# Four shared buffers, decays from ScalarE's queue, a tap on ScalarE and two moved matmul jobs in a hybrid encoder

## The chip, the cores and the metric

The kernel runs on one core of a Trainium2 chip. The metric is the device time of one execution in microseconds (us). The kernel before takes 1397.3 us, the median of three runs (1395.79 to 1398.4).

## What is computed

Two layers work on 256 tokens of width 1024 in float32. In each, one projection of the normalized input feeds three branches: a gated width-3 convolution A, a dilated attention B with 16 heads, and a bidirectional state-space branch C with 32 heads of width 64 (SSD). Their outputs go through W_a, W_b and W_c, are gated and summed ("mix"), go through W_o, and a squared-ReLU MLP follows. The parts that the change touches are these:

```
xbc = silu(depthwise_conv_centred(xbc, conv_w) + conv_b)       # 5 taps, 24 blocks of 128 channels
cum = cumsum(la, axis=2)                                       # per chunk of 128 tokens, per head
seg = cum[:, :, :, None] - cum[:, :, None, :]
decay = exp(where(tri, seg, -inf))
y_diag = einsum("bclsgr,bcsgrp->bclgrp", cb[..., None] * decay, xd)
x = x + (g_a * y_a + g_b * y_b + g_c * y_c) @ w_o
```

The kernel writes a head's SSD, both directions and both chunks, as one 256x256 matrix of decays times C·B, which multiplies x.

## The kernel before, in words

Each weight block (128x1024, 512 KB) is loaded by a request on SP's queue (`load`, L158), and is split into a rounded part wh on ScalarE and a remainder wl on VectorE (`split_to`, L173 and L174). Four raw and three split blocks are held. Three matmuls for each piece (L181, L183, L184 with 256 columns; L218 to L220 in `wide` with 512) give the product.

TensorE's order is written out by hand. `product` and `wide` call `tick()` every 12 or 6 matmuls, and small jobs (generators in `Slots`) wake at their tick: the SSD (`ssd_job`, `ssd_pair`), the attention (`attention`), and the turning of the mix (`turn_job`). A number that a job yields, or with which it is launched, is a count of ticks. The other engines' order is made by a scheduler, which puts instructions into each in-order queue by its own estimate of when they are ready.

Per layer the stages are: values; the projections with the convolutions (`conv5`); the first gate and W_a, beside which nine of the 16 pairs of SSD heads run; queries and keys with the attention; the second gate and W_b with the other seven pairs; z, the third gate and W_c; W_o; the MLP.

`conv5` (L466) sums five taps on VectorE, the centre one first (L470), into a tile cacc, of which there are two; ScalarE's Silu (L475) follows. `decays` (L477) asks for a head's summed decays in four 256 KB tiles cr through SP's queue, where weight blocks also wait. `ssd_pair` (L484) takes two heads: GpSimd adds the mask into a tile lg, of which there are two (L495); VectorE adds it to the rest of cr (L496); ScalarE takes exponentials of lg (L498) and of cr (L502, into ar); VectorE adds and multiplies them (L506, L507). Six ticks later TensorE multiplies (L512) into the one bank oy, and VectorE empties it (L516). The attention's output matmul (L642) uses the same bank, and ScalarE and VectorE empty it (L645, L646). Each group of four pairs first turns its x with two fills of the one bank pt (L534, emptied by L537), and the turning of the attention's scores uses that bank too (L631, emptied into prt by L636). `turn_job(0)` turns the first half of the mix (L717) two ticks after the first half of W_c is through, while VectorE still adds that half to the mix (L667, L668).

Of the kernel before, what the change touches and what calls it, by code (L numbers as in the profile page):

```python
# [18 lines left out]
P = 128  # L19
# [69 lines left out]
def trunk_kernel(ctx: ExitStack, tc: tile.TileContext, xT, pos, wst, wdt, small, fin, consts, out):  # L89
# [268 lines left out]
    def layer(l, xw, squares):  # L358
        prm = sm[l]

        def col(c):
            return prm[:, c : c + 1]

        st = Stream(l)
        done = set()


        uh, ul = u = big("uh"), big("ul")
# [2 lines left out]
        def norm_job():  # L371
            norm["rs"] = rs = squares.mean(D, True)
            yield 3
            pn = bcast_tokens(rs)
            for kt in range(KT):
                uf = tmp.tile([P, S], F32, name="uf", tag="cacc", bufs=2)
                DVE.scalar_tensor_tensor(uf, x[:, kt, :], col(C_MIXW + kt), pn, ALU.mult, ALU.mult)
                split_to(uh[:, kt, :], ul[:, kt, :], uf)
            if l == 0:
                rotary_tables()  # L380
            done.add("u")
# [81 lines left out]
        def xsr(ct):  # L463
            return xs[ct // 8][:, ct % 8, :]

        def conv5(raw, wct):  # L466

            acc = tmp.tile([P, S], F32, name="cacc", bufs=2)
            wc = C_SCW + 5 * wct
            DVE.tensor_scalar(acc, raw, col(wc + 2), col(C_SCB + wct), ALU.mult, ALU.add)  # L470
            for j in (0, 1, 3, 4):
                lo, hi = max(0, 2 - j), min(S, S + 2 - j)
                DVE.scalar_tensor_tensor(acc[:, lo:hi], raw[:, lo + j - 2 : hi + j - 2], col(wc + j),  # L473
                                         acc[:, lo:hi], ALU.mult, ALU.add)
            ACT.activation(raw, acc, AF.Silu)  # L475

        def decays(h):  # L477

            cr = tmp.tile([P, 4, P], F32, name="cr", bufs=CUM_BUFS)
            nc.sync.dma_start(cr.rearrange("p (d t) l -> p d (t l)", d=2),  # L480
                              ssd["cum"][h : h + 1].to_broadcast([P, 2, S]))
            return cr

        def ssd_pair(g, hp, xt, cb, ar, crs):  # L484
            bs = ssd["bs"]
            ct = 4 * g + hp
            av = []
            for j in range(2):
                h = 2 * ct + j
                cr = crs[j]  # L490
                a = ar[(2 * ct + j) % len(ar)]
                av.append(a)
                lg = tmp.tile([P, 2, P], F32, name="lg", bufs=2)

                POOL.tensor_tensor(lg, cr[:, 0::3, :], msk, ALU.add)  # L495
                DVE.tensor_tensor(cr[:, 1:3, :], cr[:, 1:3, :], msk, ALU.add)  # L496
                for t in range(2):
                    ACT.activation(lg[:, t, :], lg[:, t, :], AF.Exp,  # L498
                                   bias=bs[:, t, 32 * (1 - t) + h : 32 * (1 - t) + h + 1])

                for t in range(2):
                    ACT.activation(a[:, t * 256 : t * 256 + 256],  # L502
                                   cr[:, 2 - 2 * t : 4 - 2 * t, :].rearrange("p t l -> p (t l)"), AF.Exp,
                                   bias=bs[:, t, 32 * t + h : 32 * t + h + 1])
                ad = a.rearrange("p (q l) -> p q l", q=4)[:, 0::3, :]
                DVE.tensor_tensor(ad, ad, lg, ALU.add)  # L506
                DVE.tensor_tensor(a, a, cb, ALU.mult)  # L507
            yield Y_DELAY
            py = bank("oy", 1)
            for t in range(2):  # L510
                for j in range(2):
                    PE.matmul(py[j * 64 : j * 64 + 64, 0:256],  # L512
                              xt[:, t, hp * 128 + j * 64 : hp * 128 + j * 64 + 64],
                              av[j][:, t * 256 : t * 256 + 256], start=t == 0, stop=t == 1)
            xv = xsr(ct)
            DVE.scalar_tensor_tensor(xv, xv, col(C_SD + ct), py[:, 0:256], ALU.mult, ALU.add)  # L516
            done.add(("y", ct))

        def ssd_job():
            ar4 = big("ar", F32).rearrange("p (b c) s -> p b (c s)", b=4)  # L520
            ar2 = tmp.tile([P, 2, 512], F32, name="ar2")
            ar = [ar4[:, i, :] for i in range(4)] + [ar2[:, i, :] for i in range(2)]
            def heads(ct):
                return [decays(2 * ct + j) for j in range(2)] if ct < 16 else None

            nxt = [heads(0)]
            for g in range(4):
                bc = bcs[g]
                xt = tmp.tile([P, 2, 512], F32, name="xt", bufs=2)
                cb = tmp.tile([P, 512], F32, name="cb", bufs=2)  # L530
                for t in range(2):
                    tx = bank("pt", 1)
                    for j in range(4):
                        PE.transpose(tx[:, j * 128 : j * 128 + 128],  # L534
                                     xsr(4 * g + j)[:, t * 128 : 128 + t * 128], ident)
                    with tc.high_priority(offset=PRIO_W):
                        ACT.copy(xt[:, t, :], tx)  # L537
                    if t == 0:
                        pb = bank("s", 2)
                        for i in range(2):  # L540
                            PE.matmul(pb[:, i * 256 : i * 256 + 256], bc[:, 0, i * 128 : i * 128 + 128],
                                      bc[:, 1, :], start=True, stop=True)
                        with tc.high_priority(offset=PRIO_W):
                            ACT.copy(cb, pb)
                        yield 1
                for hp in range(4):
                    while "qk" in done and ("att", SSD_RESUME) not in done:
                        yield 1
                    crs = nxt[0]
                    nxt[0] = heads(4 * g + hp + 1)  # L550
                    slots.launch(ssd_pair(g, hp, xt, cb, ar, crs), 1)
                    yield SSD_EVERY


# [2 lines left out]
        for g in range(4):  # L557
            bc = tmp.tile([P, 2, 256], F32, name="bc", bufs=4)
            bcs.append(bc)
            ACT.copy(bc, chunks(st, 2, u))  # L560
            conv5(bc[:, 0, :], 16 + g)
            conv5(bc[:, 1, :], 20 + g)
            av = []
            for q in range(2):
                t_ = t2k("ca")
                ACT.copy(t_, chunks(st, 2, u))
                av.append(t_)
                c0 = 4 * g + 2 * q
                ACT.copy(xs[c0 // 8][:, c0 % 8 : c0 % 8 + 2, :], chunks(st, 2, u))
                for h in range(2):  # L570
                    conv5(xsr(c0 + h), c0 + h)
            bgt, ca = av
            cx = t2k("cx")
            DVE.tensor_tensor(cx, chunks(st, 2, u), ca, ALU.mult)
            for h in range(2):
                wc = C_CONVA + 3 * (2 * g + h)
                DVE.tensor_scalar(ca[:, h, :], cx[:, h, :], col(wc + 1), None, ALU.mult)
                DVE.scalar_tensor_tensor(ca[:, h, 1:S], cx[:, h, 0 : S - 1], col(wc), ca[:, h, 1:S],
                                         ALU.mult, ALU.add)
                DVE.scalar_tensor_tensor(ca[:, h, 0 : S - 1], cx[:, h, 1:S], col(wc + 2), ca[:, h, 0 : S - 1],  # L580
                                         ALU.mult, ALU.add)
            DVE.tensor_tensor(ca, ca, bgt, ALU.mult)
            split_to(ah[:, 2 * g : 2 * g + 2, :], al[:, 2 * g : 2 * g + 2, :], ca)
# [17 lines left out]
        def attention(c, qk):  # L601
# [25 lines left out]
            for j in range(2):  # L627
                tp = bank("pt", 1)
                for kb in range(2):
                    for t in range(2):  # L630
                        PE.transpose(tp[:, kb * 256 + t * 128 : kb * 256 + t * 128 + 128],  # L631
                                     scs[j][:, t, kb * 128 : kb * 128 + 128], ident)
                prt = tmp.tile([P, 512], F32, name="prt", bufs=2)
                prts.append(prt)
                with tc.high_priority(offset=PRIO_W):
                    ACT.copy(prt, tp)  # L636
                yield 2 + j
            po = bank("oy", 1)
            for kb in range(2):
                for j in range(2):  # L640
# [92 lines left out]
        def c_sink(t, c, ps):  # L733
            with tc.high_priority(offset=2 * PRIO_W if c else 0):
                add_c(t, c, ps)
            if t == 1 and c == 0:
                slots.launch(turn_job(0), 2)

        wide(st, [(ch[0], cl[0]), (ch[1], cl[1])], c_sink, 1)

# [206 lines left out]
```

## Time and profile before

| | |
|---|---|
| median of three runs | 1397.3 us |
| the profiled execution | 1397.34 us |
| its span, first to last instruction | 1395.6 us |
| mean granted TensorE clock | 0.996 |
| TensorE busy | 1362.4 us |
| VectorE busy | 1022.7 us |
| ScalarE busy | 874.4 us |

TensorE is busy in nearly all slices, so what counts is where it stands still. The two layers lie about 690 us apart: what the text says of a place at 234 us in the first layer has its counterpart near 924 us in the second.

### The profile page before, as it was taken

The numbers are of one execution on the slowest core, as the hardware profiler recorded it, in microseconds if no ns is written. First come the engines' busy times: TensorE is split into PE (matmuls) and PEld (weight loads), VectorE is DVE, ScalarE is ACT, GpSimd is POOL, SyncE is SP. The second block draws the span as 40 slices with busy tenths as digits, with TensorE's granted clock in tenths as the row PEclk, the third lists the DMA queues.
The fourth block names the chain that finished last, engine by engine and source line by source line (L and its number), as shares of the span: only waits on it lengthen the run. The fifth ranks groups of instructions, "written<-read, shape, count | busy, mean of one in ns | idle before, by whom it ended". The sixth has DMA issues, their size and how long they took to land.

```text
span 1395.6 us, 24040 instructions
## 1 busy us (share of the span) xinstructions
PE 1362.4 (98%) x9396; PEld 1229.6 (88%) x9396; DVE 1022.7 (73%) x1662; ACT 874.4 (63%) x1387; POOL 76.1 (5%) x73
## 2 busy tenths in 40 slices
PE   7999999999999999999999999999999999999997
PEld 6999986887898799999989999778878987999886
DVE  7989989975776476655579898889767765766454
ACT  6667877777576355554456687767775763555443
POOL 0000113100100000000000001220010000000000
PEclk9999999999999999999999999999999999999999
DMA  7555666534555555555555665664344555555553
GB/s 257 183 198 198 199 201 208 168 116 137 165 179 168 166 183 180 182 183 185 183 186 177 202 212 196 200 197 152 122 151 159 174 174 179 191 182 183 174 192 115
DMA packets 73698, 249.71 MB, mean 179 GB/s; under 512 B 8240, under 2 KB 8496, under 8 KB 73584
## 3 DMA queue, kind: packets, MB, share of 16 engines
q1 hardware_dynamic: 72912, 246.78, 53.9%
q8 instruction: 73, 1.20, 0.3%
q0 software_dynamic: 240, 0.77, 0.2%
q10 hardware_dynamic: 432, 0.64, 0.1%
q14 instruction: 41, 0.34, 0.1%
HBM read 246.97 MB, written 1.18 MB: 178 GB/s over the span
## 4 chain that ended last, share of the span: by engine, by line
PE 82%; DVE 9%; ACT 3%; DMA 3%; issue 2%; POOL 0%; SPq 0%; ACTq 0%; DVEq 0%; POOLq 0%
PE mm L181 16%; PE mm L184 16%; PE mm L183 16%; PE mm L218 9%; PE mm L219 9%; PE mm L220 9%; DVE wl L174 4%; DMA cr<-cumd 2%; ACT wh L173 2%; PE oy L512 2%; DVE cacc L473 1%; PE oy L642 1%; PE pt L631 1%; PE s L607 1%; DVE cr L496 0%
## 5 line engine op out<-in xcount | busy, mean ns | idle before, releaser
L174 DVE TENSOR_TENSOR wl<-raw,wh 128x1024 fp32r<-128x1024 f32 (+1 forms) x436 | 532.8, 1223 | 285.7 <-ACT wh L173 282.9
L173 ACT CAST wh<-raw 128x1024 fp32r<-128x1024 f32 (+1 forms) x436 | 454.3, 1043 | 390.5 <-PE mm L183 179.8
L181 PE MATMUL mm<-uh,wh 128*128 128x256 f32 x1296 | 371.9, 287 | 0.0
L184 PE MATMUL mm<-uh,wl 128*128 128x256 f32 x1296 | 366.9, 283 | 3.0 <-DVE wl L174 3.0
L183 PE MATMUL mm<-ul,wh 128*128 128x256 f32 x1296 | 366.6, 283 | 0.0
L181 PEld LDWEIGHTS mm<-uh,wh 128*128 128x128 f32 x1296 | 248.3, 192 | 9.6 <-issue 9.4
L184 PEld LDWEIGHTS mm<-uh,wl 128*128 128x128 f32 x1296 | 248.4, 192 | 3.8 <-DVE wl L174 3.8
L183 PEld LDWEIGHTS mm<-ul,wh 128*128 128x128 f32 x1296 | 248.5, 192 | 0.2
L183 PE MATMUL mm<-xl,wh 128*128 128x256 f32 x512 | 145.1, 283 | 0.2
L181 PE MATMUL mm<-xh,wh 128*128 128x256 f32 x512 | 145.1, 283 | 0.0
L184 PE MATMUL mm<-xh,wl 128*128 128x256 f32 x512 | 144.9, 283 | 0.0
L495 POOL TENSOR_TENSOR lg<-cr,cst 128x256 f32<-128x256 f32 x64 | 74.0, 1169 | 969.8 <-DVE cacc L473 430.9
L183 PEld LDWEIGHTS mm<-xl,wh 128*128 128x128 f32 x512 | 98.3, 192 | 0.6 <-DVE xl L281 0.6
L181 PEld LDWEIGHTS mm<-xh,wh 128*128 128x128 f32 x512 | 98.3, 192 | 0.0
L184 PEld LDWEIGHTS mm<-xh,wl 128*128 128x128 f32 x512 | 98.3, 192 | 0.0
L218 PE MATMUL mm<-wh,uh 128*128 128x512 f32 x192 | 79.5, 414 | 0.0
L219 PE MATMUL mm<-wl,uh 128*128 128x512 f32 x192 | 75.2, 392 | 0.0
L220 PE MATMUL mm<-wh,ul 128*128 128x512 f32 x192 | 75.1, 391 | 0.0
L181 PE MATMUL mm<-sh,wh 128*128 128x256 f32 x256 | 72.4, 283 | 0.0
L183 PE MATMUL mm<-sl,wh 128*128 128x256 f32 x256 | 72.4, 283 | 0.0
L184 PE MATMUL mm<-sh,wl 128*128 128x256 f32 x256 | 72.4, 283 | 0.0
L498 ACT ACTIVATE lg<-lg,bs 128x128 f32<-128x128 f32 x128 | 45.6, 396 | 39.4 <-POOL lg L495 39.0
(217 smaller groups left out, 2443.0 us busy)
## 6 DMA issues: line engine op xcount, KB each, us to landing
raw<-in_wst_dram SPq DMA_DIRECT2D x432, 512.0 KB, 3.8
cr<-cumd SPq DMA_DIRECT2D x64, 256.0 KB, 4.4
x<-in_xT_dram SPq DMA_DIRECT2D x4, 256.0 KB, 6.6
raw<-in_wdt_dram SPq DMA_DIRECT2D x2, 512.0 KB, 4.1
cst<-in_consts_dram SPq DMA_DIRECT2D x1, 706.0 KB, 8.3
finw<-in_fin_dram POOLq DMA_DIRECT2D x1, 512.0 KB, 5.3
out_dram<-xtok ACTq DMA_DIRECT2D x2, 256.0 KB, 2.6
out_dram<-xtok SPq DMA_DIRECT2D x2, 256.0 KB, 2.6
```

The costliest lines, as they stand in the source:

```text
L173: ACT.copy(dst_h, src)
L174: DVE.tensor_tensor(dst_l, src, dst_h.bitcast(F32), ALU.subtract)
L181: PE.matmul(ps, wh[:, kt, :], rh[:, kt, :], start=first and kt == kts[0], stop=False, skip_group_check=True)
L183: PE.matmul(ps, wh[:, kt, :], rl[:, kt, :], start=False, stop=False, skip_group_check=True)
L184: PE.matmul(ps, wl[:, kt, :], rh[:, kt, :], start=False, stop=last and kt == kts[-1], skip_group_check=True)
L218: PE.matmul(ps[t], rh, wh[:, k, :], start=kt == 0, stop=False)
L219: PE.matmul(ps[t], rh, wl[:, k, :], start=False, stop=False)
L220: PE.matmul(ps[t], rl, wh[:, k, :], start=False, stop=kt == rows - 1)
L473: DVE.scalar_tensor_tensor(acc[:, lo:hi], raw[:, lo + j - 2 : hi + j - 2], col(wc + j), acc[:, lo:hi], ALU.mult, ALU.add)
L495: POOL.tensor_tensor(lg, cr[:, 0::3, :], msk, ALU.add)
L498: ACT.activation(lg[:, t, :], lg[:, t, :], AF.Exp, bias=bs[:, t, 32 * (1 - t) + h : 32 * (1 - t) + h + 1])
L512: PE.matmul(py[j * 64 : j * 64 + 64, 0:256], xt[:, t, hp * 128 + j * 64 : hp * 128 + j * 64 + 64], av[j][:, t * 256 : t * 256 + 256], star ...
```

## The change

- The tile cacc, the normalization's uf and the SSD's lg now share one set of four buffers (before: two for cacc and uf together, two for lg).
- A head's decays are requested on ScalarE's queue. Two pairs are asked for when the SSD begins, and each pair asks for the second one after it, at its own end.
- The SSD's and the attention's output matmuls wait until two ticks after the last taker of bank oy.
- The mix is first turned six ticks, not two, after the first half of W_c.
- The centre tap with its bias is one ScalarE activation that reads the projection's bank, instead of a VectorE operation that reads the copy.

```
-                uf = tmp.tile([P, S], F32, name="uf", tag="cacc", bufs=2)
+                uf = tmp.tile([P, S], F32, name="uf", tag="cacc", bufs=4)
...
-            acc = tmp.tile([P, S], F32, name="cacc", bufs=2)
+            acc = tmp.tile([P, S], F32, name="cacc", bufs=4)
             wc = C_SCW + 5 * wct
-            DVE.tensor_scalar(acc, raw, col(wc + 2), col(C_SCB + wct), ALU.mult, ALU.add)
+            ACT.activation(acc, ps, AF.Identity, bias=col(C_SCB + wct), scale=col(wc + 2))
...
-            nc.sync.dma_start(cr.rearrange("p (d t) l -> p d (t l)", d=2),
+            nc.scalar.dma_start(cr.rearrange("p (d t) l -> p d (t l)", d=2),
                               ssd["cum"][h : h + 1].to_broadcast([P, 2, S]))
...
-                lg = tmp.tile([P, 2, P], F32, name="lg", bufs=2)
+                lg = tmp.tile([P, 2, P], F32, name="lg", tag="cacc", bufs=4)
...
+            ahead.append(heads(ct + 2))
             yield Y_DELAY
+            while slots.now < oy_free[0]:
+                yield 1
+            oy_free[0] = slots.now + 2
             py = bank("oy", 1)
...
-            nxt = [heads(0)]
+            ahead.extend(heads(ct) for ct in range(2))
...
-                    crs = nxt[0]
-                    nxt[0] = heads(4 * g + hp + 1)
-                    slots.launch(ssd_pair(g, hp, xt, cb, ar, crs), 1)
+                    slots.launch(ssd_pair(g, hp, xt, cb, ar, ahead.pop(0)), 1)
...
+            while slots.now < oy_free[0]:
+                yield 1
+            oy_free[0] = slots.now + 2
             po = bank("oy", 1)
...
-                slots.launch(turn_job(0), 2)
+                slots.launch(turn_job(0), 6)
```

On TensorE, at the first half of W_c's end, the order before (s is the bank of the turned mix, ch the normalized SSD output):

```order
L220 MATMUL mm<-wh,cl_4216 128x512
L717 MATMUL s<-cst,mix 128x128 x4
L218 MATMUL mm<-wh,ch_4214 128x512
L219 MATMUL mm<-wl,ch_4214 128x512
L220 MATMUL mm<-wh,cl_4216 128x512
L218 MATMUL mm<-wh,ch_4214 128x512
L219 MATMUL mm<-wl,ch_4214 128x512
L220 MATMUL mm<-wh,cl_4216 128x512
L717 MATMUL s<-cst,mix 128x128 x4
```

In the changed kernel both turnings (L727 there) stand 24 matmuls of W_c later, still six matmuls apart; nothing else moves there.

On TensorE, where the attention's last output matmul meets the tenth SSD pair, before:

```order
L642 MATMUL oy<-prt,v 64x256 x4
L512 MATMUL oy<-ar,xt 64x256 x4
L218 MATMUL mm<-wh,uh 128x512
...
L534 MATMUL pt<-cst,xs_387 128x128 x4
L541 MATMUL s<-bc 128x256 x2
L218 MATMUL mm<-wh,bh 128x512
```

and now:

```order
L652 MATMUL oy<-prt,v 64x256 x4
L218 MATMUL mm<-wh,uh 128x512
...
L541 MATMUL pt<-cst,xs_387 128x128 x4
L548 MATMUL s<-bc 128x256 x2
L522 MATMUL oy<-ar,xt 64x256 x4
L218 MATMUL mm<-wh,bh 128x512
```

The SSD pair's matmul moved behind twelve projection matmuls and the turning of x. The eleventh pair moved back by six. Elsewhere TensorE's order is the same.

On ScalarE, from the attention's first exponentials (scr the scores, prt the turned ones), before:

```order
L620 ACTIVATE scr,den<-scr,mx 128x256 x2
L624 ACTIVATE scr<-scr,rden 128x256
L173 CAST wh<-raw 128x1024
L624 ACTIVATE scr<-scr,rden 128x256
L620 ACTIVATE scr,den<-scr,mx 128x256 x2
L624 ACTIVATE scr<-scr,rden 128x256 x2
L173 CAST wh<-raw 128x1024
L636 COPY prt<-pt 128x512
```

and now:

```order
L627 ACTIVATE scr,den<-scr,mx 128x256 x2
L631 ACTIVATE scr<-scr,rden 128x256
L173 CAST wh<-raw 128x1024
L631 ACTIVATE scr<-scr,rden 128x256
L627 ACTIVATE scr,den<-scr,mx 128x256 x2
L508 ACTIVATE ar<-cr,bs 128x256 x2
L631 ACTIVATE scr<-scr,rden 128x256 x2
L508 ACTIVATE ar<-cr,bs 128x256 x2
L173 CAST wh<-raw 128x1024
L643 COPY prt<-pt 128x512
L627 ACTIVATE scr,den<-scr,mx 128x256 x2
L481 DMA cr<-cumd 128x512
```

Up to the attention's fourth pair, ScalarE's queue now holds eight exponentials of cr, eight of lg and four requests that stood ahead of the attention, or on SP's queue, before. Between the first turning of x and this place it holds 19 requests, eight more exponentials of lg and four fewer of cr. Over the whole program ScalarE's table loads fall from 60 to 44.

## Rows read from the trace of the kernel before

**Rows 1.** The page's parts 1 and 4: busy time; the chain by engine.

```profile
PE 1362.4 (98%) x9396; PEld 1229.6 (88%) x9396; DVE 1022.7 (73%) x1662; ACT 874.4 (63%) x1387; POOL 76.1 (5%) x73
PE 82%; DVE 9%; ACT 3%; DMA 3%; issue 2%; POOL 0%; SPq 0%; ACTq 0%; DVEq 0%; POOLq 0%
```

**Rows 2.** TensorE's waits: for whom, us in total, times, longest us.

```profile
PE mm L218 <- ACT wh L173: 6.7, 1, 6.7
PE pt L534 <- ACT xt L537: 5.2, 2, 3.2
PE s L717 <- DVE mix L668: 4.6, 4, 1.9
PE mm L184 <- DVE wl L174: 3.0, 4, 0.8
PE oy L512 <- DVE bl L646: 1.9, 2, 0.9
PE pt L631 <- ACT prt L636: 1.7, 2, 1.6
```

**Rows 3.** Stretches: us, busy us of each engine, PEclk, DMA share, GB/s.

```profile
470.20:473.40 3.20, 3.20 (x11) 2.50 (x11) 1.11 (x2) 0.60 (x1) 0.00 (x0) 0.50 0.41 145
927.60:930.80 3.20, 3.20 (x13) 1.60 (x12) 2.97 (x7) 2.79 (x7) 0.00 (x0) 0.50 0.62 202
```

**Rows 4.** Stretches: convolutions; first gate and W_a; the attention's first chunks, both layers.

```profile
60.00:184.00 124.00, 122.47 (x999) 121.15 (x999) 109.50 (x193) 90.31 (x129) 10.60 (x8) 1.00 0.60 198
184.00:262.00 78.00, 75.92 (x448) 60.46 (x448) 70.81 (x118) 55.89 (x112) 21.97 (x18) 1.00 0.60 201
262.00:296.00 34.00, 32.24 (x253) 27.73 (x250) 29.11 (x86) 27.87 (x69) 0.00 (x0) 1.00 0.38 126
950.50:985.00 34.50, 34.40 (x276) 30.83 (x274) 30.82 (x93) 27.59 (x68) 0.00 (x0) 1.00 0.40 133
```

**Rows 5.** ScalarE's and VectorE's groups: count, busy, mean ns, idle before.

```profile
L502 ACT ACTIVATE ar<-cr,bs 128x256 f32<-128x256 f32 x128 | 55.7, 499 | 3.8 <-PE oy L512 3.7
L498 ACT ACTIVATE lg<-lg,bs 128x128 f32<-128x128 f32 x128 | 45.6, 396 | 39.4 <-POOL lg L495 39.0
L475 ACT ACT_TABLE_LOAD x18 | 23.1, 1283 | 14.9 <-DVE cacc L473 14.7
L470 DVE TENSOR_SCALAR cacc<-xs,sm 128x256 f32<-128x256 f32 x32 | 11.7, 408 | 0.0
L470 DVE TENSOR_SCALAR cacc<-bc,sm 128x256 f32<-128x256 f32 x16 | 7.7, 511 | 0.0
```

**Rows 6.** Timeline ahead of the wait at 234 us: start us, us, instruction, idle before.

```profile
229.63 1.70 ACT L502 ACTIVATE ar<-cr,bs 128x256 f32<-128x256 f32 x4
233.57 0.69 ACT L498 ACTIVATE lg<-lg,bs 128x128 f32<-128x128 f32 x2 [2.24 <-POOL lg L495]
234.17 1.03 ACT L173 CAST wh<-raw 128x1024 fp32r<-128x1024 f32 x1
235.11 0.58 ACT L537 COPY xt<-pt 128x512 f32<-128x512 f32 x1
232.35 1.87 POOL L495 TENSOR_TENSOR lg<-cr,cst 128x256 f32<-128x256 f32 x2 [4.30 <-DVE ar L506]
```

**Rows 7.** VectorE and TensorE at the mix's first turning.

```profile
467.05 1.22 DVE L174 TENSOR_TENSOR wl<-raw,wh 128x1024 fp32r<-128x1024 f32 x1
468.18 0.68 DVE L668 TENSOR_TENSOR mix<-mix,gc 128x512 f32<-128x512 f32 x1
468.92 0.55 PE L717 MATMUL s<-cst,mix 128*128 128x128 f32 x3 [1.91 <-DVE mix L668]
```

**Rows 8.** Requests: ScalarE's own (ns min/median/max); the decays' landing; SP's wait.

```profile
L349 ACTq DMA_DIRECT2D out_dram<-xtok x2: 338/342/345, 1388.6 to 1391.8; - x2
cr<-cumd SPq DMA_DIRECT2D x64, 256.0 KB, 4.4
SPq L480 <- ACT ar L502: 30.7, 27, 3.6
```

More of the change, by code (lines that the diff above doesn't have):

```diff
@@ L365, in layer @@
         done = set()
+        oy_free = [0]
         uh, ul = u = big("uh"), big("ul")
@@ L464, in xsr, with conv5 @@
             return xs[ct // 8][:, ct % 8, :]
-        def conv5(raw, wct):
-            acc = tmp.tile([P, S], F32, name="cacc", bufs=2)
+        def conv5(raw, ps, wct):
+            acc = tmp.tile([P, S], F32, name="cacc", bufs=4)
             wc = C_SCW + 5 * wct
-            DVE.tensor_scalar(acc, raw, col(wc + 2), col(C_SCB + wct), ALU.mult, ALU.add)
+            ACT.activation(acc, ps, AF.Identity, bias=col(C_SCB + wct), scale=col(wc + 2))
             for j in (0, 1, 3, 4):
@@ L479, in decays, with heads @@
             cr = tmp.tile([P, 4, P], F32, name="cr", bufs=CUM_BUFS)
-            nc.sync.dma_start(cr.rearrange("p (d t) l -> p d (t l)", d=2),
+            nc.scalar.dma_start(cr.rearrange("p (d t) l -> p d (t l)", d=2),
                               ssd["cum"][h : h + 1].to_broadcast([P, 2, S]))
             return cr
+        def heads(ct):
+            return [decays(2 * ct + j) for j in range(2)] if ct < 16 else None
+        ahead = []
         def ssd_pair(g, hp, xt, cb, ar, crs):
@@ L522, in ssd_job @@
             ar = [ar4[:, i, :] for i in range(4)] + [ar2[:, i, :] for i in range(2)]
-            def heads(ct):
-                return [decays(2 * ct + j) for j in range(2)] if ct < 16 else None
-            nxt = [heads(0)]
+            ahead.extend(heads(ct) for ct in range(2))
             for g in range(4):
@@ L559, in layer @@
             bcs.append(bc)
-            ACT.copy(bc, chunks(st, 2, u))
-            conv5(bc[:, 0, :], 16 + g)
-            conv5(bc[:, 1, :], 20 + g)
+            y = chunks(st, 2, u)
+            ACT.copy(bc, y)
+            conv5(bc[:, 0, :], y[:, 0, :], 16 + g)
+            conv5(bc[:, 1, :], y[:, 1, :], 20 + g)
             av = []
@@ L568, in layer @@
                 c0 = 4 * g + 2 * q
-                ACT.copy(xs[c0 // 8][:, c0 % 8 : c0 % 8 + 2, :], chunks(st, 2, u))
+                y = chunks(st, 2, u)
+                ACT.copy(xs[c0 // 8][:, c0 % 8 : c0 % 8 + 2, :], y)
                 for h in range(2):
-                    conv5(xsr(c0 + h), c0 + h)
+                    conv5(xsr(c0 + h), y[:, h, :], c0 + h)
             bgt, ca = av
```

## The prediction

> **What bounds the kernel now.** I read the page's busy times and chain first, then TensorE's waits, then single places in the timeline. TensorE is busy for 1362.4 of 1395.6 us, and it holds 82% of the chain that ends last [rows 1]. So VectorE's and ScalarE's busy time counts only where TensorE stands still for it, and the list of TensorE's waits is the list of all that can be won [rows 2]. The reader sees there six kinds of gap: 6.7 us once for the first weight block, which nothing here touches, and five that the edits touch: 5.2 us in two for the turned x, 4.6 us in four for the mix, 3.0 us in four for the remainder wl, 1.9 us in two for bank oy, 1.7 us in two for the turned scores. They come to 16.4 us. After two of these gaps the clock is granted at 0.50, which is 1.2 GHz instead of 2.4: in 470.2 to 473.4 us behind the mix's gap, and in 927.6 to 930.8 us behind the second layer's gap for x [rows 3]. In these 3.2 us TensorE does 1.6 us of work, so each costs 1.6 us more. The other layer's gaps of the same kinds had no such stretch in their place. Everything beyond 16.4 + 3.2 = 19.6 us is TensorE's own work, which the change leaves as it is: only the places of a few matmuls change.
>
> The sum is made against the profiled execution, 1397.34 us, 1.7 us of it around the span; the median shown is 1397.3, the same.
>
> **Centre tap.** Per layer VectorE loses 16 operations of 408 ns and 8 of 511 ns [rows 5]: 6.5 + 4.1 = 10.6 us of the 109.5 us that it is busy in the convolution stage of 124 us [rows 4]. ScalarE gains 24 activations of 256 columns. The trace has none that reads a bank with two column operands; the nearest is the exponential of cr with one column, 499 ns alone [rows 5] and 1.70 us for four in a row, 0.43 each [rows 6]. I take 0.5: 12 us on an engine busy for 90.3 of 124 [rows 4]. Against that ScalarE loses table loads, 60 to 44 in all, eight per layer of 1283 ns [rows 5], 10.3 us. It stays near 92 of 124. So the four gaps for wl go, which are 0.8 us at most each [rows 2], while two taps are 0.8 us and VectorE passes several pairs between two gaps: -3.0 us, between 0 and -3.0.
>
> The Trainium skill speaks against this edit: "ScalarE: Activation LUTs", Rules for kernel authors, sends multiplications and additions to VectorE. Singly this trace agrees with it, 408 against about 499 ns [rows 5]. By the rule the tap would be a loss; here VectorE is the fuller engine, and the sum above does not follow it.
>
> **lg in four buffers, decays from ScalarE's queue.** The 234 us gap shows the chain [rows 6]. ScalarE ends its exponentials of cr at 231.33, then stands still for 2.24 us for GpSimd's lg; GpSimd itself had stood still for 4.30 us, until VectorE had read the previous lg, and started at 232.35. Behind the waiting exponential in ScalarE's queue stand a weight cast of 1.03 us and the copy of x at 235.11, and TensorE waits for that copy. With four buffers GpSimd need not wait for that reader. I expect the two gaps and the half clock behind the second to go: -5.2 - 1.6 = -6.8 us, between 0 and -6.8. The request itself asks for the same four cr tiles: it can't leave before the last reader two pairs back is done. SP waited 30.7 us for just that reader [rows 8]; on ScalarE's queue the request stands behind it anyway and adds no long wait. What it adds is its issue: 338 to 345 ns for ScalarE's own requests [rows 8], 0.34. Weight casts, exponentials and copies are queued behind it. Landing, 4.4 us [rows 8], stays hidden.
>
> "DMA: Bandwidth & Descriptors", Issuing engines are not separate DMA queues, in the Trainium skill says that requests of all engines run on the same 16 DMA engines, so that another issuer saves only the time to start them. By it nothing is won in landing, and what is won must come from the buffers alone. No row shows a decay from another queue.
>
> **What ScalarE then does later.** By its new order it holds, in the first gate and W_a, 8 more lg exponentials (0.69 us for two [rows 6], 2.8), 4 fewer of cr (-1.7) and 19 requests (6.5): +7.6, so 55.9 becomes 63.5 us against TensorE's 75.9 us of work [rows 4]. VectorE, at 70.8, gets no more. Cover enough: 0.
>
> In the attention's first chunks the cover is gone. The queue gains 8 exponentials of cr (3.4), 8 of lg (2.8) and 4 requests (1.4), 7.6 us. There ScalarE is busy for 27.87 us beside TensorE's 32.24 in the first layer, and 27.59 beside 34.40 in the second [rows 4]. It becomes 35.5 and 35.2: over by 3.2 and 0.8 us, where 1.8 (34.00 - 32.24) and 0.1 us of gaps stand now. That is +2.1 us for both layers, if ScalarE never waits. It does wait here, for maxima and sums from VectorE. The bounds are -1.8 (it has run ahead, and the gap for the scores closes) and +13.4 (all 15.2 us on TensorE's path, less the 1.8 there now). I take +4.5, nearer the lower end, because ScalarE's idle time there, 6.1 us in the first layer, takes most of the 7.6.
>
> **Bank oy in turns.** TensorE's wait for VectorE's emptying, 1.9 us in two [rows 2], is filled with twelve matmuls. A 256-column matmul takes 0.12 us (999 in 122.47 [rows 4]) and these, of 512, no less: over 1.4 us, against 0.9 each. -1.9 us, between 0 and -1.9; the pairs behind it move back by at most one turn.
>
> **Mix turned later.** 1.91 us of TensorE's standing is for VectorE's second addition at 468.18, behind a wl of 1.22 us [rows 7]. Now 24 matmuls, over 2.9 us, stand in front. Two waits of 1.9 go, the two short ones at the second turning (0.4 each by difference) stay, and the half clock of 470 us goes: -3.8 - 1.6 = -5.4, between 0 and -5.4. The turned half is needed only at W_o, after the rest of W_c.
>
> uf in four buffers lies in the value stage, where TensorE has no wait: 0 either way, at most some tenths.
>
> **Sum:** -3.0 - 6.8 + 4.5 - 1.9 - 5.4 = -12.6, so 1397.3 - 12.6 = 1384.7 us.
>
> **Rivals.**
>
> Nothing crowds: ScalarE's later work fits into its idle time, and the score gaps close as well. -17.1 - 1.8 = -18.9, 1378.4 us. For it: ScalarE stands still for 39.0 us in all for GpSimd's lg [rows 5], which four buffers can give back. Against it: the order puts the eight exponentials among the attention's first ones.
>
> The gap for x stays, because ScalarE's queue still reaches the copy of x late: cr has four tiles as before, so "two pairs ahead" may ask no sooner, and a late landing holds GpSimd as the buffer did. Then 6.8 us are not won: 1397.3 - 5.8 = 1391.5 us. By the skill's rule on issuing engines this is the way it would go, if the decays' landing were what counts; the row has GpSimd released by VectorE's reading, with the decays of that head there [rows 6].
>
> Slower: ScalarE's in-order queue becomes the bound. Place: first gate and W_a. There 63.5 us of work plus its standing for GpSimd, 39.0 / 2 = 19.5 us a layer if four buffers do not shorten it, is 83.0 against 75.9: 7.1 a layer, 14.2 in the place of 5.2. All 15.2 us of the attention's extra come on the path as well, as the same queue arrives late there. The gains of the tap, oy and the mix are 3.0 + 1.9 + 5.4 = 10.3. 1397.3 - 10.3 + 9.0 + 15.2 = 1411.2 us. It decides from the point where new gaps exceed the 17.1 us of gains. Against it: in the convolution stage ScalarE's work does not grow, and most of its standing was for the buffer that is now doubled.
>
> **How the numbers follow.** Forecast 0.45, no crowding 0.25, the x gap stays 0.20, slower 0.10. A difference under 0.2% (2.8 us) can't be told from none here. The forecast and the first rival lie far above that. The second is at 5.8 us, and more crowding than I took brings a quarter of it within the bound or beyond: 0.05. Of the slower case, milder forms fall within the bound: 0.02. So faster 0.85, same 0.07, slower 0.08. The forecast's own range is 1380 to 1390. The range with 8 in 10 starts at the first rival, 1377.5, and goes past the second to 1395, leaving out the slower case and a little of each end.
>
> **What would show it.** In the changed kernel's list of TensorE's waits: no wait for wl in the convolutions (tap), none for mix over 0.5 us, none for VectorE at oy, none for the copy of x; the clock at 1.00 after the second layer's W_a and in W_c; waits for the turned scores of some 1 to 4 us a layer in the attention's first chunks, with ScalarE busy there without a break. ScalarE's standing for GpSimd's lg should fall well under 39.0 us. It is wrong if the gap for x stays with GpSimd released by a decay's landing, or if TensorE waits for weight casts in the first gate and W_a.

## The result and the profile after

The changed kernel takes 1382.15 us (median of 4, 1381.86 to 1384.98) against 1396.55 us for the kernel before beside it (4 runs, 1394.17 to 1398.4). The ratio is 0.9905, with a 95% interval of 0.9892 to 0.9918. The medians are 14.4 us apart. The two profiled executions, from which the terms are read, are 12.4 us apart: 1397.34 and 1384.98 us. The latter is the slowest of its four, with a span of 1383.2 us. The forecast was 12.6 us. The total is right; two of its reasons are not.

The page's parts 1 and 4 of the changed kernel, in the place of [rows 1]:

```profile
PE 1360.0 (98%) x9396; PEld 1228.5 (89%) x9396; DVE 1010.8 (73%) x1614; ACT 877.2 (63%) x1419; POOL 71.2 (5%) x73
PE 89%; DVE 6%; ACT 2%; issue 1%; DMA 1%; ACTq 0%; DVEq 0%; POOLq 0%
```

TensorE's work is the same within 2.4 us, and its part of the last chain grew from 82 to 89%: what went was its standing still. Its waits (for whom, us in total, times, longest us), against [rows 2]:

```profile
PE mm L218 <- ACT wh L173: 6.7, 1, 6.7
PE pt L638 <- ACT prt L643: 5.7, 6, 1.4
PE mm L219 <- DVE wl L174: 1.0, 1, 1.0
PE s L727 <- DVE mix L678: 0.8, 2, 0.4
PE oy L522 <- DVE ar L513: 0.4, 1, 0.4
PE pt L638 <- ACT scr L631: 0.3, 2, 0.2
PE oy L522 <- DVE xs L526: 0.2, 1, 0.2
```

Of the five kinds of gap that the edits touch, four have gone or shrunk. The two for x and the four for wl in the convolutions are no longer there; the one wl left is at the kernel's start. The mix keeps its two short ones. At bank oy there are 0.6 us of another kind: 0.4 for VectorE's products (ar, L513) and 0.2 for its emptying of the bank after an earlier pair (L526). The fifth has grown: the waits for the turned scores went from 1.7 to 5.7 us. By stretch (us, busy us of PE, PEld, VectorE, ScalarE and GpSimd, granted clock, DMA share, GB/s), against [rows 4]:

```profile
60.00:184.00 124.00, 124.00 (x1009) 122.79 (x1009) 101.83 (x171) 87.51 (x129) 4.99 (x5) 1.00 0.56 189
258.00:292.00 34.00, 31.89 (x251) 27.71 (x252) 33.82 (x95) 29.83 (x78) 3.26 (x4) 1.00 0.47 153
941.50:976.00 34.50, 32.35 (x254) 27.83 (x253) 33.78 (x96) 30.57 (x77) 3.13 (x4) 1.00 0.46 153
```

The first row is the convolutions, and there TensorE no longer stands still at all. The other two are the attention's first chunks, which begin some 4 us earlier in the first layer now. TensorE loses 2.1 us in each. VectorE is full, 33.82 of 34.00 us; ScalarE is not, with 29.83. In the groups of part 5 (count, busy us, mean ns, idle before) the rows that answer to [rows 5] are:

```profile
L508 ACT ACTIVATE ar<-cr,bs 128x256 f32<-128x256 f32 x128 | 58.7, 501 | 1.5 <-PE oy L522 1.4
L504 ACT ACTIVATE lg<-lg,bs 128x128 f32<-128x128 f32 x128 | 44.7, 393 | 5.9 <-ACT ar L508 3.2 <-POOL lg L501 2.6
L471 ACT ACTIVATE cacc<-mm,sm 128x256 f32<-128x256 f32 x48 | 24.6, 568 | 0.0
```

ScalarE's standing for GpSimd's lg fell from 39.0 to 2.6 us. The tap, whose price no row of before had, takes 568 ns, where 500 had been taken.

### The profile page after: what moved, and what is told of

Read it like the earlier page. It is cut to its first block, busy times and chain, and to the rows that moved or that the text cites. A ratio compares the mean times of both kernels' runs of the same rounds, so it can differ in the third digit from the quotient of the medians.

```text
span 1383.2 us, 24009 instructions
## 1 busy us (share of the span) xinstructions
PE 1360.0 (98%) x9396; PEld 1228.5 (89%) x9396; DVE 1010.8 (73%) x1614; ACT 877.2 (63%) x1419; POOL 71.2 (5%) x73
## 4 chain that ended last, share of the span: by engine, by line
PE 89%; DVE 6%; ACT 2%; issue 1%; DMA 1%; ACTq 0%; DVEq 0%; POOLq 0%
PE mm L181 17%; PE mm L183 17%; PE mm L184 17%; PE mm L218 11%; PE mm L219 11%; PE mm L220 10%; PE oy L522 2%; DVE wl L174 2%; PE oy L652 1%; ACT wh L173 1%; DMA cr<-cumd 1%; PE pt L638 1%; PE pt L541 1%; DVE scr L623 1%; PE s L548 1%
## 5 line engine op out<-in xcount | busy, mean ns | idle before, releaser
L501 POOL TENSOR_TENSOR lg<-cr,cst 128x256 f32<-128x256 f32 x64 | 69.1, 1090 | 963.8 <-ACT xs L476 671.2
L508 ACT ACTIVATE ar<-cr,bs 128x256 f32<-128x256 f32 x128 | 58.7, 501 | 1.5 <-PE oy L522 1.4
```

The source lines that it names most:

```text
L508: ACT.activation(a[:, t * 256 : t * 256 + 256], cr[:, 2 - 2 * t : 4 - 2 * t, :].rearrange("p t l -> p (t l)"), AF.Exp, bias=bs[:, t, 32 * ...
```

## The experiments

Each kernel ran five rounds against the kernel before on the same chip. Kernels on different chips are compared by their ratios to it.

| kernel | what it is | us, median (range) | ratio, 95% |
|---|---|---|---|
| u_tap | after, tap on VectorE | 1380.51 (1378.99–1381.52) | 0.9895 [0.9878, 0.9912] |
| u_buf | after, two buffers | 1378.15 (1377.90–1378.70) | 0.9880 [0.9864, 0.9896] |
| u_queue | after, requests on SP | 1403.02 (1401.04–1404.47) | 1.0055 [1.0041, 1.0070] |
| u_mix | after, mix early | 1388.30 (1386.66–1392.68) | 0.9949 [0.9934, 0.9965] |
| q_oy_mix | after, two buffers, tap on VectorE | 1381.97 (1381.38–1384.91) | 0.9908 [0.9895, 0.9920] |
| o_queue | before, ScalarE's queue, two ahead | 1388.93 (1387.19–1390.51) | 0.9952 [0.9939, 0.9964] |
| o_buf | before, four buffers | 1408.36 (1407.30–1410.02) | 1.0093 [1.0079, 1.0107] |
| hold4 | after, late pairs held back | 1378.97 (1378.45–1379.11) | 0.9880 [0.9867, 0.9894] |
| o_engine | before, ScalarE's queue, one ahead | 1388.86 (1388.79–1390.91) | 0.9954 [0.9941, 0.9967] |
| o_ahead | before, SP's queue, two ahead | 1394.83 (1392.82–1397.34) | 0.9999 [0.9990, 1.0009] |
| u_buf_hold | u_buf, held to the 5th pair | 1378.60 (1378.40–1380.36) | 0.9880 [0.9865, 0.9894] |
| u_buf_hold5 | u_buf, held to the 6th pair | 1383.41 (1381.96–1384.31) | 0.9910 [0.9896, 0.9925] |

### Buffers or queue: which of them closes the gap for x

**u_buf** takes the four buffers out of the changed kernel.

```diff
-uf tag="cacc", bufs=4;  cacc bufs=4;  lg tag="cacc", bufs=4
+uf tag="cacc", bufs=2;  cacc bufs=2;  lg bufs=2
```

> The changed kernel with cacc and uf in two buffers and lg in two of its own, as before. Own theory (GpSimd waited for the reader of lg): the gaps for the turned x come back, 5.2 to 6.8 us, ScalarE stands still for lg some 39 us again, and some 1388 us. Rival (the tap's relief of VectorE or the decays' queue closed those gaps): no gap for x over 0.5 us, ScalarE's standing for lg well under 39 us, 1382 us.

**u_queue** keeps the buffers and gives the requests back to SP, still two pairs ahead.

```diff
-nc.scalar.dma_start(cr...)
+nc.sync.dma_start(cr...)
```

> The changed kernel with the decays requested on SP's queue again, two pairs ahead. Own theory: the gaps for the turned x stay closed; ScalarE saves 32 issues of 0.33 us a layer, of which only those in the attention's first chunks lie where TensorE waits, so the waits for the turned scores (5.7 us) fall by 0 to 2.5 us: 1380 to 1382.5 us. Rival (the queue closed the gaps for x): gaps of 5.2 us and slower by 5 to 7 us, 1387 to 1389 us.

The answer is the opposite of the prediction. Without the four buffers the kernel is faster still, 1378.15 us, and its list of TensorE's waits has none for x. Besides the two waits at the kernel's start it holds:

```profile
PE pt L638 <- ACT prt L643: 1.8, 2, 0.9
PE s L727 <- DVE mix L678: 0.8, 2, 0.4
```

Without ScalarE's queue it is slower than the kernel before, though the four buffers are there, and the gaps for x are the largest wait:

```profile
PE pt L541 <- ACT xt L544: 13.9, 4, 5.2
```

How the first of them comes about is in u_queue's timeline (start us, us, engine, line, instruction, idle before and its releaser), here rows of ScalarE, SP, GpSimd and TensorE in order of time:

```profile
202.56 1.71 ACT L508 ACTIVATE ar<-cr,bs 128x256 f32<-128x256 f32 x4
203.54 0.33 SPq L481 DMA_DIRECT2D cr<-cumd  x1
204.43 0.38 SPq L481 DMA_DIRECT2D cr<-cumd  x1
207.22 0.92 POOL L501 TENSOR_TENSOR lg<-cr,cst 128x256 f32<-128x256 f32 x1 [5.94 <-DMA cr<-cumd]
208.17 0.40 ACT L504 ACTIVATE lg<-lg,bs 128x128 f32<-128x128 f32 x1 [2.68 <-POOL lg L501]
212.56 0.57 ACT L544 COPY xt<-pt 128x512 f32<-128x512 f32 x1
213.18 1.12 PE L541 MATMUL pt<-cst,xs 128*128 128x128 f32 x4 [5.12 <-ACT xt L544]
```

Read it upwards: TensorE waits for ScalarE's copy of x; that copy stands behind an exponential of lg that waited 2.68 us for GpSimd; GpSimd waited 5.94 us for a decay's landing, not for a buffer of lg; and that decay was asked for, at 203.54 us, as soon as the first two of ScalarE's block of four exponentials had read its tile of cr.

**o_queue**, **o_buf**, **o_engine** and **o_ahead** do single parts from the side of the kernel before. o_queue sends the requests from ScalarE two pairs ahead (the change's `ahead` list and `nc.scalar.dma_start`, nothing else that moves work); o_engine moves them alone, with `nxt` one pair ahead as before; o_ahead has the list alone, on SP; o_buf has the three `bufs=4` alone.

```diff
# o_engine, one line
-nc.sync.dma_start(cr...)
+nc.scalar.dma_start(cr...)
```

> The kernel before with one edit: the decays requested on ScalarE's queue, two pairs ahead. New theory: the gaps for x (5.2 us and a half clock of 1.6) go, perhaps those for wl too (3.0); those for the mix (4.6 and 1.6) and at oy (1.9) stay: 6.8 to 10 us faster than before, ratio 0.993 to 0.995. Rival (the request needs the late turns or the buffers to be worth anything): within 2 us of before.

> The kernel before with one edit: cacc, uf and lg in one set of four buffers. The theory of the prediction (GpSimd waited for lg's reader): the gaps for x go, 5 to 7 us faster. New theory (in one set with cacc the lg tiles come only behind all convolutions, so the SSD starts without its lead, and requests on SP's queue come late): gaps of about 5 us for x in each layer and stretches at half clock, 8 to 16 us slower, ratio 1.006 to 1.012.

> The kernel before with the decays requested on ScalarE's queue and still one pair ahead. Theory (which queue the request stands in decides): as with both, 1387 to 1390 us, no gap for x or wl. Rival (the second pair ahead decides): gaps for x of 4 us and more, 1393 to 1397 us.

> The kernel before with the decays still on SP's queue, asked for two pairs ahead. Theory (there are four tiles in either case, and the request stands behind weight blocks): within 2.8 us of before, gaps for x of 4 us and more. Rival (the second pair ahead decides): no gap for x, 1387 to 1390 us.

The queue alone wins 6.5 us (1388.86, ratio 0.9954), the distance alone nothing (0.9999), and both together no more than the queue (0.9952). The waits of o_engine:

```profile
PE s L717 <- DVE mix L668: 4.6, 4, 1.9
PE pt L631 <- ACT prt L636: 4.1, 3, 2.0
PE oy L512 <- DVE bl L646: 1.9, 2, 0.9
```

x and the convolutions' wl have gone; the mix and oy stand as in [rows 2], since o_engine leaves them alone. The waits for the scores are 4.1 us, where they were 1.7: the queue alone brings much of what crowds the attention's first chunks. In o_ahead the wait for x stays at 4.7 us:

```profile
PE pt L538 <- ACT xt L541: 4.7, 2, 2.5
```

Whether lg's buffer had anything to do with it is in the groups of o_engine:

```profile
L495 POOL TENSOR_TENSOR lg<-cr,cst 128x256 f32<-128x256 f32 x64 | 85.0, 1335 | 958.8 <-DMA cr<-cumd 516.6 <-DVE ar L506 402.2 <-DVE mx L618 13.8
L498 ACT ACTIVATE lg<-lg,bs 128x128 f32<-128x128 f32 x128 | 45.3, 395 | 17.6 <-POOL lg L495 16.7 <-ACT ar L502 0.8
```

GpSimd still stands 402.2 us for VectorE's reading of lg, with the same two buffers; the kernel before has 413.0 us there. Yet ScalarE's standing for lg falls from 39.0 to 16.7 us, and the gap is gone. So the buffer that the row at 232.35 us names [rows 6] was not what made x late.

Nor were SP's requests late. Counted from the records, a decay's request leaves SP 0.09 us in the median after the last reader of its tile in the kernel before, and 0.74 us after it on ScalarE's queue in o_engine (56 requests each, those that have a reader before them). Nor do weight blocks come late behind them on SP's queue: ScalarE's casts stand 0.9 us in all for a block's landing in the kernel before, and 0.5 in o_engine. What the queue changes is ScalarE's order. A request in its stream stands behind the exponentials of its own head, and the scheduler, which writes the engines' orders when the kernel is built, then does head by head what it had done in pairs. o_engine's timeline of ScalarE around its copy of x, where the kernel before has one block of four and then a wait [rows 6]:

```profile
225.98 0.91 ACT L502 ACTIVATE ar<-cr,bs 128x256 f32<-128x256 f32 x2
226.80 0.39 ACT L498 ACTIVATE lg<-lg,bs 128x128 f32<-128x128 f32 x1
226.92 0.33 ACTq L480 DMA_DIRECT2D cr<-cumd  x1
227.38 0.90 ACT L502 ACTIVATE ar<-cr,bs 128x256 f32<-128x256 f32 x2
229.99 0.58 ACT L537 COPY xt<-pt 128x512 f32<-128x512 f32 x1
```

Counted over the whole run, the exponentials of cr stand in ScalarE's stream like this (single ones, threes and fives left out):

| kernel | requests from | blocks of two | blocks of four | waits for x, us |
|---|---|---|---|---|
| before | SP | 6 | 24 | 5.2 |
| o_ahead | SP | 6 | 24 | 4.7 |
| o_buf | SP | 6 | 28 | 12.4 |
| u_queue | SP | 4 | 28 | 13.9 |
| o_engine, o_queue, q_oy_mix | ScalarE | 38 | 6 | none |
| u_tap | ScalarE | 44 | 6 | none |
| u_buf | ScalarE | 36 | 6 | none |
| after | ScalarE | 32 | 8 | none |

TensorE's own order is the same in o_engine as in the kernel before, row for row. A block of four stands behind the lg exponentials of both its heads. So both tiles come free late and close together (u_queue's two requests above leave 0.89 us apart), the lg that need the new decays come late, and ScalarE waits. That the queue's edit closes the gap is shown; that it does so by this order, and not in another way, is argued from these counts: no kernel with ScalarE's requests and blocks of four was run. (The two kernels that hold pairs back in u_buf have 0.6 and 0.3 us of waits for x, once each, and no others of ScalarE's have any.)

o_buf is the other half. The four shared buffers alone cost 13 us (1.0093). Its waits for x are 12.4 us:

```profile
PE pt L534 <- ACT xt L537: 12.4, 4, 4.8
```

and GpSimd's first lg in its timeline starts at

```profile
166.65 2.50 POOL L495 TENSOR_TENSOR lg<-cr,cst 128x256 f32<-128x256 f32 x2 [164.01 <-ACT xs L475]
```

In the kernel before the first one starts at 96.58 us, behind a decay's landing. With one set of buffers under one name, lg gets its turn only behind the convolution's sums that are asked for ahead of it (L475 is the activation that reads them). The scan (the SSD's pairs) loses 70 us of its lead; u_queue, with the same buffers, starts at 166.66 us. Pairs that have no lead feel every late block, so u_queue and o_buf have gaps of 5.1 and 4.8 us at 208 us, where the kernel before has none. With ScalarE's queue the four buffers cost only the 4.0 us between the changed kernel and u_buf (0.9905 and 0.9880: the intervals overlap a little, the times' ranges do not). And they cost that only beside the tap on ScalarE: with the tap on VectorE, four buffers (u_tap, 0.9895) and two (q_oy_mix, 0.9908) can't be told apart.

### The tap

**u_tap** puts it back on VectorE; **q_oy_mix** does this and takes out the buffers as well.

```diff
-ACT.activation(acc, ps, AF.Identity, bias=..., scale=...)
+DVE.tensor_scalar(acc, raw, col(wc + 2), col(C_SCB + wct), ALU.mult, ALU.add)
```

> The changed kernel with the centre tap back on VectorE; all else as changed. Own theory (each edit closes its own gaps): TensorE waits for wl again in the convolutions, four times, 3.0 us, and for nothing else that is new: some 1385 us against the changed kernel's 1382.2. Rival (VectorE's relief by the tap is what closed the gaps for the turned x as well): those two gaps of 5.2 us and a half clock come back too, 9.8 us in all, some 1392 us.

> The changed kernel without two of its edits at once: centre tap back on VectorE, cacc, uf and lg in two buffers each as before; the decays from ScalarE's queue, the turns at oy and the late turn of the mix stay. New theory (the decays' request on ScalarE's queue closes the gaps for x and for wl; tap and buffers close none): no gap for x or wl over 0.5 us, waits for the turned scores of some 1.8 us as without the buffers, 1376 to 1380 us. Rival (tap and buffers each hid the other's absence, one of them is needed): the four wl gaps (3.0 us) or the x gaps (5.2 us and more) come back, 1381 to 1387 us.

u_tap can't be told from the changed kernel: 0.9895 and 0.9905, with intervals that overlap. Its convolution stage reads

```profile
60.00:184.00 124.00, 124.00 (x1010) 122.81 (x1009) 109.04 (x193) 78.60 (x109) 4.12 (x4) 1.00 0.57 189
```

VectorE is as busy there as in the kernel before (109.04 and 109.50 us), and TensorE still never waits. So the tap isn't needed for the gaps for wl to go. They go in o_engine too, where VectorE has even more, 111.77 us. And they go in o_buf, which has the buffers alone: TensorE is busy for 124.00 of the 124 us there, with VectorE at 109.07 and GpSimd at 4.88, where it had 10.60, since the scan begins so late. Either of these edits is enough; the tap alone was not run. With two buffers the tap does win: u_buf against q_oy_mix is 1378.15 against 1381.97 us (0.9880 and 0.9908; the intervals just touch), with no run of the one within the range of the other. q_oy_mix lies in its rival's range of 1381 to 1387 us, but not for the rival's reason: neither the gaps for wl nor those for x came back. What differs in TensorE's waits is again the scores, 1.8 against 3.8 us, and one stretch at half clock, behind q_oy_mix's wait of 1.91 us at 955.51 us. In 258 to 292 us VectorE has 30.53 us in u_buf and 31.68 in q_oy_mix; it seems to have got ahead with the scan's pairs when the convolutions left it room, but no run shows that apart.

### The mix

**u_mix** turns it at 2 ticks again.

```diff
-slots.launch(turn_job(0), 6)
+slots.launch(turn_job(0), 2)
```

> The changed kernel with the mix turned two ticks after the first half of W_c, as before. Own theory: two waits of 1.9 us for VectorE's addition come back, with or without a stretch at half clock behind one of them: 3.8 to 5.4 us slower than 1382.2, 1386 to 1387.6 us. Rival (the wait was an echo of VectorE's lateness further up, now relieved): no wait over 0.5 us there, 1382 us.

1388.30 us, 6.2 more than the changed kernel. Its waits have `mix` at 4.6 us in four, as in [rows 2], and behind each of the long ones, in both layers, the clock falls to the lower level (columns as in the stretches above):

```profile
467.70:470.80 3.10, 3.10 (x11) 2.51 (x10) 1.04 (x2) 0.60 (x1) 0.00 (x0) 0.50 0.36 140
1153.70:1156.90 3.20, 3.20 (x11) 2.51 (x11) 0.69 (x1) 0.60 (x1) 0.00 (x0) 0.50 0.55 198
```

Two waits of 1.9 us and two such stretches at 1.6 us each are 7.0 us; the profiled executions are 7.7 apart. That execution of u_mix is the slowest of its six, and the 6.2 us of the medians lie between one stretch (5.4) and two.

### The attention's first chunks

**hold4** makes the scan's pairs from the tenth on wait until the attention's fifth pair, by an operand that is only ready then; **u_buf_hold** does the same in u_buf, **u_buf_hold5** at the sixth pair.

```diff
+mk = ssd["late"] if ct >= 9 else msk
-POOL.tensor_tensor(lg, cr[:, 0::3, :], msk, ALU.add)
+POOL.tensor_tensor(lg, cr[:, 0::3, :], mk, ALU.add)
-DVE.tensor_tensor(cr[:, 1:3, :], cr[:, 1:3, :], msk, ALU.add)
+DVE.tensor_tensor(cr[:, 1:3, :], cr[:, 1:3, :], mk, ALU.add)
...
+ssd["late"] = ...   # msk * rden, at c == 4 and j == 0
```

> The changed kernel with the SSD pairs from the tenth on held back until the attention's fifth pair: their mask is a copy multiplied by a reciprocal sum of that pair (positive, so the masked places stay masked and the others 0), one VectorE operation of 128x256 more a layer. Theory (the preparation of pairs ten to twelve, pulled in among the attention's first chunks, fills VectorE there and makes the waits for the turned scores): these waits fall from 5.7 us to under 2 us, and the time by 3 to 5 us, to 1377 to 1379 us. Rival (the waits come from the attention's own chain, exponentials and copies in series): they stay at 4 us or more, 1381 to 1383 us.

> The changed kernel with the buffers as before (two and two) and the SSD pairs from the tenth on held back until the attention's fifth pair. Theory (both leave VectorE room in the attention's first chunks; together no wait of the turned scores is left there): waits for turned scores under 1.5 us in all, 1376 to 1378.5 us. Rival (the held pairs crowd the later chunks instead): waits of 2 us and more around the fifth and sixth pair, 1378 to 1381 us.

> As the one before, held back until the attention's sixth pair. Theory: the later the hold, the less there is left to wait for as long as the tenth pair's product is ready by the attention's end: waits for turned scores under 1 us, 1375.5 to 1378 us. Rival: the tenth to twelfth pair are late, TensorE waits for ar or the turned x behind the attention, 1379 us and more.

hold4 wins 3.2 us on the changed kernel (1378.97 us; the ratios are 0.9880 and 0.9905, whose intervals overlap a little, while the times' ranges do not). Its first chunks read

```profile
258.00:292.00 34.00, 34.00 (x274) 30.39 (x272) 29.26 (x82) 27.32 (x67) 3.32 (x4) 1.00 0.39 126
```

VectorE has 4.6 us less than in the changed kernel, ScalarE 2.5, and TensorE no gap in the stretch; the waits for the scores are 2.3 us in all, later, not quite under the 2 us expected. So it is the moved pairs that make most of the 4.0 us by which these waits had grown. In u_buf, where these waits are 1.8 us already, holding them wins nothing (1378.60 and 1378.15), and a pair later it loses 5 us: the pairs held back are then late themselves.

```profile
PE oy L523 <- DVE xs L527: 2.8, 2, 1.6
```

This row is u_buf_hold5's; u_buf_hold has none for oy. Its waits for the scores are 0.8 us longer as well (2.1 against 1.3); the rest of its loss is open.

The fastest version is u_buf, with u_buf_hold and hold4 level. It beats the kernel before by 1.2% and the changed one by 4.0 us.

## Why the prediction was right, and where it was wrong

By the profiled executions, term by term:

| step | forecast | by the waits and stretches |
|---|---|---|
| wl in the convolutions | -3.0 | -3.0 |
| x, with the half clock | -6.8 | -6.8 |
| attention's first chunks | +4.5 | +4.3 (1.7 to 5.7 and 0.3) |
| bank oy | -1.9 | -1.3 (0.6 new) |
| mix, with the half clock | -5.4 | -5.4 |
| sum | -12.6 | -12.2; measured -12.4 |

By the medians the measured change is -14.4 us. The clock, in the places where it was granted at 0.50 before [rows 3], is at 1.00 now:

```profile
464.00:480.00 16.00, 16.00 (x76) 13.27 (x75) 8.52 (x10) 6.47 (x8) 0.00 (x0) 1.00 0.51 173
927.00:940.00 13.00, 13.00 (x104) 11.79 (x103) 13.00 (x26) 8.07 (x18) 2.41 (x3) 1.00 0.62 194
```

**The step that failed is the cause of the x gap.** The prediction said: "what is won must come from the buffers alone", and of the request that on ScalarE's queue it "adds no long wait" and is otherwise only 0.34 us more to issue. The runs show the reverse: the queue wins 6.5 us alone, and the buffers lose 13 alone. That the term of -6.8 us came out is luck: by the prediction's reasoning u_queue, which has the buffers, would have no gap for x, and it has 13.9 us of them. What I had read of the requests holds: they wait for just the reader that [rows 8] names, and SP sends them at once. Two things were not asked. The first is what else an instruction does that is put into an engine's stream: it changed how the 128 exponentials of cr are grouped around it. The prediction counted how many of them move to a later stage, and gave the request a price of 0.34 us, but did not ask how they are grouped. The second is whether the releaser in [rows 6] is a cause. In o_engine GpSimd stands for that reader almost as long (402.2 against 413.0 us), and the gap is gone.

The Trainium skill's rule, "DMA: Bandwidth & Descriptors", Issuing engines are not separate DMA queues, agrees with this case: landing took 4.4 us before and takes 4.2 after, and in o_engine the requests leave no sooner behind their reader for the new issuer. From that rule I concluded that the buffers must be what wins, and this did not follow from it.

The rival "the gap for x stays" named the late landing that u_queue then has, and cr's four tiles as its reason; but with ScalarE's requests the same four tiles are enough. The slower rival, ScalarE's queue as the bound in the first gate and W_a, did not come: TensorE has no wait for a weight cast there.

**The request's price was too high in most places.** ScalarE's timeline in the changed kernel:

```profile
202.91 1.06 ACT L173 CAST wh<-raw 128x1024 fp32r<-128x1024 f32 x1 [0.24 <-PE mm L220]
202.92 0.33 ACTq L481 DMA_DIRECT2D cr<-cumd  x1
203.87 0.50 ACT L508 ACTIVATE ar<-cr,bs 128x256 f32<-128x256 f32 x1
```

The request is issued while the cast runs, and the next instruction follows without a break, as it does at 40 of the 64 requests. Where the request waits for the very exponential ahead of it, ScalarE does pay:

```profile
212.35 0.51 ACT L508 ACTIVATE ar<-cr,bs 128x256 f32<-128x256 f32 x1
212.89 0.33 ACTq L481 DMA_DIRECT2D cr<-cumd  x1
213.26 0.69 ACT L504 ACTIVATE lg<-lg,bs 128x128 f32<-128x128 f32 x2 [0.40 <-ACT ar L508]
```

Eight exponentials of lg stand 0.40 us in this way, which is the 3.2 us in the row of L504 above, and two casts 0.45. That is some 4 us in all, where 64 requests at 0.34 would be 22.

**Tap: the size right, the reason not.** ScalarE's stage has 87.51 us, where I said near 92; VectorE's fell by 7.7, not 10.6. But the four gaps for wl go without it, by the queue alone and by the buffers alone. One of the two of each layer stands, in the trace of before, behind the scan's own bunching:

```profile
164.19 1.97 DVE L496 TENSOR_TENSOR cr<-cr,cst 128x256 f32<-128x256 f32 x4
166.08 1.21 DVE L174 TENSOR_TENSOR wl<-raw,wh 128x1024 fp32r<-128x1024 f32 x1
```

Four additions in a row stand ahead of the wl for which TensorE then waits 0.81 us. In o_engine these additions come as one at 160.41 us and two at 169.48. In o_buf none stands in that place. The other gap, at 116.6 us, has no work of the scan near it on VectorE; why it goes is open, and no run changes the order of VectorE alone.

**The attention: the size right, the engine half right.** The +4.5 was worked out from ScalarE alone: 7.6 us more on it. It got 2 to 3 us more, and it is VectorE that became full, of whose share of the moved pairs the prediction says nothing there. Both are in the first gap, before TensorE goes on at 265.89 us: ScalarE had waited 1.05 us for VectorE's reciprocal until 259.18, and then worked without a break until its copy of the scores:

```profile
259.18 0.51 ACT L631 ACTIVATE scr<-scr,rden 128x256 f32<-128x256 f32 x1 [1.05 <-DVE rden L629]
261.92 0.90 ACT L508 ACTIVATE ar<-cr,bs 128x256 f32<-128x256 f32 x2
263.52 0.90 ACT L508 ACTIVATE ar<-cr,bs 128x256 f32<-128x256 f32 x2
265.26 0.58 ACT L643 COPY prt<-pt 128x512 f32<-128x512 f32 x1
```

The two pairs of decay exponentials in front are 1.8 us, the gap is 1.38. hold4 takes the pairs away from both engines, so it shows that they are the cause, not which engine counts more. (The range's lower end, 1377.5, is called the first rival's; that rival's own sum is 1378.4.)

**Oy and mix as told, but for a remainder.** u_mix undoes the mix and loses what it was to win. Oy alone was not undone; o_queue and o_engine, without the turns, keep its 1.9 us, and the changed kernel, u_buf and hold4, with them, have no wait for the attention's emptying. The sign "none for VectorE at oy" is not quite met in the changed kernel, by the 0.6 us of its other waits there.

## What to carry to other kernels

A request that is moved into a computing engine's stream is an edit of that engine's order; compare the order before and after at the place that waits, and how many like operations stand there in a block, before any price is given to the request. More buffers under a shared name can take a stage's lead away, because they are handed out in the program's order; give a stage that is to run ahead its own. When several edits go together and the total comes out as forecast, undo each: here the shared buffers, beside the tap, cost some 4 us, and two kinds of gap went by other edits than the ones meant for them.

## What the runs showed of the hardware

VectorE's addition of the mask to the decays had a mean of 471 ns before and has 569 now; by its own line (ns, least, median and most) in the changed kernel:

```profile
L502 DVE TENSOR_TENSOR cr<-cr,cst x64: 397/422/971, 96.8 to 1034.8; 128x256 f32<-128x256 f32 x64
```

Counted over the records of both lines, the 31 of the 64 that don't overlap with an lg of GpSimd take 413 ns in the mean and 428 at most; the 33 that do take 714. Which of the two starts first decides: the 9 that began before the lg took 413 to 426 ns; the 20 that began while an lg was running took 580 to 971, and ended 0.28 us after it. The other 4, of 411 to 414 ns, lie inside the two longest lg, of 3.7 and 3.8 us. In the kernel before 23 overlap, with a mean of 570. Both engines' additions read two tiles in SBUF. The Trainium skill, "SBUF — State Buffer", SBUF: two separate sides, has a rule for just this pair, by which the later of the two waits until the first is done; the 29 of the first two kinds agree with it, and whether the two long lg are GpSimd's own waiting isn't shown. The change made this dearer: a decay's landing, which VectorE's addition waits for as well, releases GpSimd's lg 33 times now, and twice before.

The same gap does not always bring the same clock. In o_engine the mix's wait of 1.9 us stands in both layers; after the first one the clock is granted at 0.50, which is 1.2 GHz, and after the second it stays at 1.00:

```profile
465.20:468.40 3.20, 3.20 (x11) 2.54 (x10) 0.69 (x1) 0.68 (x2) 0.00 (x0) 0.50 0.48 160
1151.30:1154.50 3.20, 3.20 (x18) 2.71 (x19) 0.90 (x2) 1.20 (x2) 0.00 (x0) 1.00 0.56 200
```

In 3.2 us there are 11 matmuls in the one and 18 in the other. u_mix has the lower level after both. So such a stretch, 1.6 us, is a term that follows the same gap in one place and not in another. Each kernel has one trace, so whether it also changes between executions of one kernel is not shown. A forecast to better than that isn't to be had from one profile.
